# Conformer norm of a decoder trunk: the statistic as four columns, one unit further down, with some of its squares added on GpSimd

## The chip, the cores and the metric

One NeuronCore of a Trainium2 chip runs the whole kernel. The metric is the device time of one execution in microseconds; the time before is the median of three runs. A core has five engines that matter here: PE (TensorE; its weight loads are listed as PEld), DVE (VectorE), ACT (ScalarE), POOL (GpSimd) and SP (SyncE, which here only issues DMAs).

## The reference, cut to what matters

The reference is a trunk of two layers over 512 positions with 1024 channels. Layer 0 mixes tokens with a gated DeltaNet, layer 1 with a Conformer convolution module; each layer then attends to a fixed memory and applies a squared-ReLU MLP. Every sub-layer has an RMS norm before it and a residual add behind it.

```
def rms_norm(x, g):
    y = xf * lax.rsqrt(jnp.mean(xf * xf, axis=-1, keepdims=True) + RMS_EPS)
    return (y * g).astype(x.dtype)

def conformer_conv(h, w_pw1, b_pw1, w_dw, b_dw, ln_g, ln_b, w_pw2, b_pw2):
    u = h @ w_pw1 + b_pw1
    u = u[..., :D_MODEL] * jax.nn.sigmoid(u[..., D_MODEL:])
    c = causal_depthwise_conv(u, w_dw) + b_dw
    c = jax.nn.silu(layer_norm(c, ln_g, ln_b))
    return c @ w_pw2 + b_pw2
```

The change concerns the RMS norm ahead of `conformer_conv`: the mean over 1024 channels of h squared, for each of 512 tokens.

## The kernel before, in words

Activations lie with channels on the 128 partitions and the 512 tokens along a tile: a layer's state h is eight tiles of 128x512. Each operand of a matmul is split into a rounded part and a remainder (xh and xl, wh and wl; type fp32r), and a product is three matmuls of 512 columns, `mm3` (L290: lines 292, 293, 294). A projection `proj` (L300) runs `mm3` over the eight k tiles into one PSUM bank: 24 matmuls, called a unit here.

The norm's gain is folded into xh and xl (`Norm.parts`, L376: xh on ACT, xl on DVE). Its scale per token, rb, comes later: the projections run on unscaled x, and the result is multiplied by rb when it is taken out of PSUM. `Norm.square` (L383) squares an h tile on ACT (sq) and adds it to the running sum; the last add is on DVE. When all eight are in, `split` (L329) makes sqh and sql. `Norm.stat` (L395) multiplies both by a 128x128 matrix of ones, which sums over the partitions and leaves the sum in all 128 rows (ssq), takes the root of all 128x512 on ACT (sd) and the reciprocal on DVE (rb). Another way stands in the class and serves the first norm of the kernel: `stat_tok` (L404) takes root and reciprocal of a column for each 128 tokens (128x4, rstd), and `spread` (L410) spreads the four columns by four PE transposes (`spread_t`, L359) and a copy on ACT to rb.

The stretch in question is the end of layer 0's MLP and the start of the Conformer. `outs` (L1183) transposes the MLP's result back: four PSUM banks hT by 16 transposes, then for each tile h = hT + residual on DVE and `parts`. It is called for tiles 0 to 3 ahead of the last product of the MLP, and for tiles 4 to 7 (`rest`) inside the Conformer's first unit. Behind tile 7 it squares all eight h, with the adds on DVE.

`conformer` (L1266) begins with the first pointwise projection. `pw_mm` (L1274) runs unit (m, half): half 0 is the value and half 1 the gate of channel tile m. Unit (0, 0) does k 0 to 3, then `rest`, then unit (0, 1) does k 0 to 3, then both do k 4 to 7; inside the last of these, behind k = 5, stands `norm.stat`. `pw_ev` (L1285) scales by rb, applies the sigmoid and makes the gated tile: the sigmoid on ACT, the rest on DVE. Then come the convolutions: tile 0 has its 31 taps on ACT and GpSimd (cvp, ca), tiles 1 to 4 on DVE (L1350, one instruction for a tap), tiles 5 to 7 on PE (L1413). The projections of the memory's keys and values (K, V) fill PE meanwhile, in the order of `CONV_SEQ` and `CONV_AFTER` (L1732). The LayerNorm is taken on DVE (L1391 to L1438), and `ln_out` (L1442) transposes back on PE (lnT) for the second pointwise projection.

The order of the instructions on each engine is fixed when the kernel is built: a scheduler goes by the order of the program and by its own estimate of when operands are ready, so neighbouring units may be mixed. Each engine then runs its list strictly in that order and waits on semaphores. Weights come as raw tiles by SP's DMAs; `wsplit` (L241) makes wh on ACT and wl on DVE (some on GpSimd) two units ahead, in a ring of three (NW). PSUM has eight banks.

Of the kernel before, what the change touches and what calls it, by code (L numbers as in the profile page):

```python
# [11 lines left out]
ALU = mybir.AluOpType  # L12
AX = mybir.AxisListType

P = 128
# [22 lines left out]
def tile_trunk(ctx, tc, xT, memT, x_d, mem_d, prm_d, adt_d, bdw_d, tap_d, fin_d, w_ab, w_kq, w_v, w_z, w_dno, w_pw1, w_pw2,  # L38
               w_q, w_k, w_vv, w_o, w_up, w_dn, yT):
    nc = tc.nc  # L40
    pe, act, dve, pool = nc.tensor, nc.scalar, nc.vector, nc.gpsimd
# [10 lines left out]
    def nm(s):  # L52
        cnt[0] += 1
        return f"{s}_{cnt[0]}"

    def slot(dt=F32, s="u", shape=(P, NT)):
        return up.tile(list(shape), dt, tag="u", name=nm(s))

    def psum(s="ps"):
        return psp.tile([P, NT], F32, tag="ps", name=nm(s))  # L60
# [4 lines left out]
    def const(shape, s, dt=F32):  # L65
        return cp.tile(list(shape), dt, tag=s, name=s)
# [3 lines left out]
    def tt(e, o, a, b, op):  # L70
        r = e.tensor_tensor(out=o, in0=a, in1=b, op=op)  # L71
        if e is pool:
            last_pool[:] = [r]
        return r

    def stt(o, a, s, b, op0, op1):
        return dve.scalar_tensor_tensor(out=o, in0=a, scalar=s, in1=b, op0=op0, op1=op1)  # L77
# [7 lines left out]
    def c4(t):  # L85
        return t.rearrange("p (c i) -> p c i", c=4)
# [9 lines left out]
    def pc(name, i=0):  # L96
        return (gn0 if name == "dn_norm" else prm)[:, OFF[name] + i:OFF[name] + i + 1]
# [28 lines left out]
    ones = const([P, P], "ones")  # L126
# [137 lines left out]
    def wnext(key, hf):  # L264
        i = ws["next"]
        assert order[i] == (key, hf), (order[i], key, hf)
        while ws["load"] <= need[min(i + NRAW + 1 + 2 * (order[i][0][0] in ("up", "dn7")), len(order) - 1)]:
            wload()
        while ws["split"] < min(i + (NW if i > 2 else (1, 2, 2)[i]), len(order)):
            wsplit()  # L270
        ws["next"] += 1
        return ws["hl"].pop(i)
# [17 lines left out]
    def mm3(ps, wk, xk, first, last):  # L290
        (wh, wl), (xh, xl) = wk, xk
        pe.matmul(ps, wh, xh, start=first, stop=False)  # L292
        pe.matmul(ps, wh, xl, start=False, stop=False)  # L293
        pe.matmul(ps, wl, xh, start=False, stop=last)  # L294

    def wk(w, k):
        c = slice(k * P, (k + 1) * P)
        return w[0][:, c], w[1][:, c]

    def proj(w, xs, ps, k0=0, k1=KT, inside=None):  # L300
        for k in range(k0, k1):
            mm3(ps, wk(w, k), xs[k], k == 0, k == KT - 1)
            if inside and k in inside:
                inside[k]()
# [24 lines left out]
    def split(src, s):  # L329
        h = slot(F32R, s + "h")  # L330
        act.copy(h, src)  # L331
        lo = slot(F32R, s + "l")
        tt(dve, lo, src, h.bitcast(F32), ALU.subtract)
        return h, lo
# [32 lines left out]

    class Norm:
        def __init__(self, gname):
            self.g, self.acc, self.xs, self.n = gname, None, [], 0  # L370

        def add(self, t, h):
            self.parts(t, h)
# [6 lines left out]
            pin(stt(xl, h, pc(self.g, t), xh.bitcast(F32), ALU.mult, ALU.subtract))  # L380
            self.xs.append((xh, xl))

        def square(self, h, e=pool):  # L383
            sq = slot(s="sq")
            act.activation(sq, h, AF.Square)  # L385
            self.n += 1
            if self.acc is None:
                self.acc = sq
            else:
                tt(dve if self.n == KT else e, self.acc, self.acc, sq, ALU.add)  # L390
            if self.n == KT:
                self.hl = split(self.acc, "sq")

        def stat(self):
# [676 lines left out]
    def mlp7(layer, norm, hres, nxt=None, mid=None):  # L1071
        xs = norm.xs
# [108 lines left out]
        new = [None] * 8  # L1181

        def outs(tiles):  # L1183
            todo = [(n, c, i) for n in range(2) for c in range(2) for i in tiles]
            pss = {i: psum("hT") for i in tiles}
            for n, c, i in todo:
                j = 2 * n + c
                pe.transpose(pss[i][:, j * P:(j + 1) * P], acc[n, 1 - i // 4, c][:, i % 4 * P:i % 4 * P + P], ident)
            for k, i in enumerate(tiles):
                hn = slot(s="h")  # L1190
                tt(dve, hn, pss[i], hres[i], ALU.add)
                new[i] = hn
                if k:
                    nxt.parts(i - 1, new[i - 1])
            nxt.parts(i, hn)
            if i == 7:
                for hn in new:
                    nxt.square(hn, dve)

        def final(n, m, c):  # L1200
            opens = n not in fin or fin[n][4][c] is None
# [26 lines left out]
        for g in range(4):  # L1228
            ops, us = [{} for _ in range(4)], []
            for i in range(8):  # L1230
                w = wnext(("up", layer, g * 4 + i // 2), i % 2)
                ps = psum("up")
# [33 lines left out]
    def conformer(norm, hres, nxt, rest):  # L1266
        xs = norm.xs
        st, xg = {}, {}
        bn = slot(s="bn")
        Y = [[slot(s="cy") for _ in range(2)] for _ in range(4)]  # L1270
        for y in Y:
            nc.sync.dma_start(out=y[1], in_=bdw_d[512:1024].partition_broadcast(P))

        def pw_mm(m, hf):  # L1274
            w, st[m, hf] = wnext(("pw1", m), hf), psum("pw")
            if m:
                return proj(w, xs, st[m, hf])
            proj(w, xs, st[m, hf], 0, 4)
            if hf == 0:
                st["w"] = w  # L1280
                return rest()
            proj(st.pop("w"), xs, st[0, 0], 4, 8)
            proj(w, xs, st[0, 1], 4, 8, inside={5: norm.stat})

        def pw_ev(m):  # L1285
            sg = slot(s="sg")
            tt(dve, sg, st.pop((m, 1)), norm.rb, ALU.mult)
            act.activation(sg, sg, AF.Sigmoid, bias=pc("b_pw1", 8 + m))
            a = slot(s="pa")
            tt(dve, a, st.pop((m, 0)), norm.rb, ALU.mult)  # L1290
            if m == 0:
                x4 = c4(wp.tile([P, 544], F32, tag="cv", name=nm("xp"), bufs=NCV))
                pool.memset(x4[:, :, 0:8], 0.0)
                stt(x4[:, :, 8:136], c4(a), pc("b_pw1", m), c4(sg), ALU.add, ALU.mult)
                todo_p.extend(pool_conv(m, x4))
                return
            if m < NTAP:
                x7 = fsp.tile([P, 1024], F32, tag="fs", name=nm("x7"))[:, 0:1008].rearrange("p (q t) -> p q t", q=7)
                pool.memset(x7[:, :, 0:10], 0.0)
                stt(x7[:, 3:7, 8:136], c4(a), pc("b_pw1", m), c4(sg), ALU.add, ALU.mult)  # L1300
                act.copy(x7[:, 0:3, 9:137], x7[:, 4:7, 8:136])
                todo.extend(dve_conv(m, x7))
                return
            x = wp.tile([P, 544], F32, tag="cv", name=nm("xg"), bufs=NCV)
            x4 = c4(x)
            pool.memset(x4[:, :, 0:8], 0.0)
            gl = slot(s="glu")
            stt(gl, a, pc("b_pw1", m), sg, ALU.add, ALU.mult)
            for j in range(4):
                for b in range(4):  # L1310
                    nc.sync.dma_start(out=x4[32 * b:32 * b + 32, j, 8:136],
                                      in_=gl[32 * j:32 * j + 32, 128 * b:128 * b + 128])
            xg[m] = x4
# [64 lines left out]
        def taps_pool(n):  # L1378
            for _ in range(min(len(todo_p), n)):
                todo_p.pop(0)()  # L1380

        def taps_dve(n):
            for _ in range(min(len(todo), n)):
                todo.pop(0)()
# [76 lines left out]
        for i, (kind, u) in enumerate(CONV_SEQ):  # L1461
            if kind == "p":
                m, hf = divmod(u, 2)
                pw_mm(m, hf)
                if hf == 1:
                    pw_ev(m)
            else:
                kv_unit(1, u)

            for ins in gate:  # L1470
                stack.enter_context(tc.issue_after(ins.ins))
            taps_dve(TAPS_U[i])
            stack.close()
            taps_pool(2 if kind == "p" else 1)
            for what, m, *js in after.pop(i, ()):
                {"t": taps, "c": lambda m: conv(m, js), "l": lambda m: ln(), "s": lambda m: root_table(), "o": ln_out, "d": turn,
                 "m": lambda m: behind(first["tap"], moments, m)}[what](m)
                if what == "c":
                    for ins in gate:
                        stack.enter_context(tc.issue_after(ins.ins))  # L1480
                    taps_dve(TAPS_C[m])
                    stack.close()
                taps_pool(3 if what == "c" else 0)
            gate = [x for x in (ws["ins"], mem.get("kf")) if x is not None] if i >= 15 else []
        assert not after
        new = []
        for m in range(8):
            ps = psum("pw2")
            proj(wnext(("pw2", m // 2), m % 2), ss, ps)
            hn = slot(s="h")  # L1490
# [114 lines left out]
    for gq in range(2):  # L1605
# [9 lines left out]
        for i in range(4):  # L1615
            h = 4 * gq + i
# [50 lines left out]
    h = []  # L1667
# [13 lines left out]
    h = xattn(0, n1, h, n2)  # L1681
    n3 = Norm("cv_norm")
    h, rest = mlp7(0, n2, h, n3, lambda: (mem_gain(1, 0), mem_gain(1, 1), taps(NTAP)))
    n4 = Norm("xa_norm1")
    h = conformer(n3, h, n4, rest)
    n5 = Norm("mlp_norm1")
    h = xattn(1, n4, h, n5)
# [149 lines left out]
```

## Time and profile before

| | |
|---|---|
| runs, us | 1472.95, 1472.52, 1470.46 (median 1472.52) |
| profiled execution, us | 1472.31 |
| its span, us | 1470.6 |
| granted TensorE clock, mean of the span | 0.998 |
| DVE add `h<-hT,h`, 8 in the kernel | 684 ns each |
| DVE reciprocal of 128x512 (L401), 5 in the kernel | 3353 ns each |

The profile is taken from one execution. The span is from its first to its last instruction; the time of the execution also has what lies around it. Busy times are per engine; PE's matmuls are pipelined, so the distance between starts (0.23 us for 512 columns) and not the listed duration (0.39) is what one costs in a stream. A row gives start, duration, engine, line, operation and tiles (out<-in); in brackets stands how long the engine sat idle before it, and what ended that. Lists of a tile give duration in ns as min/median/max. Line numbers are those of the kernel before.

### The profile page before, as it was taken

The page shows a single profiled execution, that of the slowest core. Times are in us where ns is not written, and L with a number is a line of the kernel's source. Part 1 is how long each engine was busy: PE and PEld are TensorE (multiplying, and loading weights), DVE is VectorE, ACT ScalarE, POOL GpSimd, SP SyncE. Part 2 cuts the span into 40 slices and gives each one's busy share as a digit, 9 for nine tenths or more (in the row PEclk, how much of TensorE's full clock was granted, in tenths as well). Part 3 has the DMA queues.
Part 4 walks back from the last instruction along what each step waited for, and adds up shares of the span by engine and source line. Part 5 has one row for each costly group of instructions (what it writes and reads, how often), then busy time and mean ns, then how long its engine had stood idle before and what let it go on. Part 6 is the DMA issues. An engine that isn't in the chain of part 4 may idle for free.

```text
span 1470.6 us, 19621 instructions
## 1 busy us (share of the span) xinstructions
PE 1454.7 (99%) x7298; PEld 1226.6 (83%) x7298; DVE 1068.6 (73%) x1619; ACT 771.8 (52%) x1326; POOL 261.0 (18%) x285
## 2 busy tenths in 40 slices
PE   9999999999999999999999899999999999999998
PEld 7888889988888888888888689988888888888886
DVE  5889889867646766767679799985555766767677
ACT  7765865655434554444354655464444544444354
POOL 1411310103113000000000387302113000000100
PEclk9999999999999999999999999999999999999999
DMA  7232124342213666574766424432204466574853
GB/s 272 94 115 72 58 86 156 131 144 87 73 43 114 158 172 175 142 201 136 203 163 219 151 87 164 171 139 101 72 34 131 138 170 179 138 212 126 232 144 86
DMA packets 62736, 201.83 MB, mean 137 GB/s; under 512 B 7728, under 2 KB 10032, under 8 KB 62640
## 3 DMA queue, kind: packets, MB, share of 16 engines
q1 hardware_dynamic: 52416, 164.39, 31.7%
q0 software_dynamic: 9792, 35.66, 14.0%
q8 instruction: 57, 0.93, 0.2%
q10 hardware_dynamic: 432, 0.52, 0.1%
q14 instruction: 39, 0.32, 0.1%
HBM read 197.66 MB, written 2.10 MB: 136 GB/s over the span
## 4 chain that ended last, share of the span: by engine, by line
PE 92%; DVE 3%; ACT 2%; DMA 1%; issue 1%; SPq 0%; POOL 0%; DVEq 0%; ACTq 0%
PE up L294 8%; PE up L293 8%; PE up L292 8%; PE dn L1123 6%; PE dn L1121 6%; PE dn L1122 6%; PE pw L293 3%; PE pw L294 3%; PE pw L292 3%; PE h L292 2%; PE h L293 2%; PE h L294 2%; PE xo L293 2%; PE q L292 2%; PE q L293 2%; PE q L294 2%
## 5 line engine op out<-in xcount | busy, mean ns | idle before, releaser
L251 ACT CAST wh<-raw 128x1024 fp32r<-128x1024 f32 x259 | 272.0, 1052 | 356.5 <-issue 96.7
L71 DVE TENSOR_TENSOR wl<-raw,wh 128x1024 fp32r<-128x1024 f32 (+1 forms) x250 | 305.7, 1225 | 104.1 <-ACT wh L251 98.2
L292 PE MATMUL up<-xh,wh 128*128 128x512 f32 x512 | 199.7, 390 | 0.0
L294 PE MATMUL up<-xh,wl 128*128 128x512 f32 x512 | 199.3, 389 | 0.0
L293 PE MATMUL up<-xl,wh 128*128 128x512 f32 x512 | 199.2, 389 | 0.0
L293 PEld LDWEIGHTS up<-xl,wh 128*128 128x128 f32 x512 | 96.1, 188 | 20.0
L294 PEld LDWEIGHTS up<-xh,wl 128*128 128x128 f32 x512 | 96.1, 188 | 19.9
L292 PEld LDWEIGHTS up<-xh,wh 128*128 128x128 f32 x512 | 96.1, 188 | 19.8
L239 POOL DMA_DIRECT2D t<-w_dn x48 | 42.2, 917 | 360.9 <-DVE wl L71 239.8
L1121 PE MATMUL dn<-wh,ah 128*128 128x512 f32 x256 | 99.8, 390 | 0.0
L1123 PE MATMUL dn<-wl,ah 128*128 128x512 f32 x256 | 99.6, 389 | 0.0
L1122 PE MATMUL dn<-wh,al 128*128 128x512 f32 x256 | 99.6, 389 | 0.0
L77 DVE SCALAR_TENSOR_TENSOR rl<-up,rb 128x512 f32<-128x512 f32 x64 | 44.2, 690 | 58.2 <-PE up L294 58.2
L1350 DVE SCALAR_TENSOR_TENSOR ca<-x,prm,ca 128x512 f32<-128x512 f32 x112 | 82.3, 754 | 3.6 <-ACT ca L1347 1.3
L251 ACT CAST wh<-t 128x1024 fp32r<-128x1024 f32 x44 | 46.5, 1056 | 55.5 <-PE dn L1122 43.7
L71 DVE TENSOR_TENSOR wl<-t,wh 128x1024 fp32r<-128x1024 f32 x44 | 53.7, 1224 | 29.2 <-ACT wh L251 29.1
L292 PE MATMUL h<-xh,wh 128*128 128x512 f32 x184 | 73.7, 400 | 0.0
L294 PE MATMUL h<-xh,wl 128*128 128x512 f32 x184 | 71.9, 391 | 0.0
L293 PE MATMUL h<-xl,wh 128*128 128x512 f32 x184 | 71.7, 390 | 0.0
L71 DVE TENSOR_TENSOR acc<-acc,dn 128x512 f32<-128x512 f32 x100 | 67.4, 683 | 1.1
L71 POOL TENSOR_TENSOR sq<-sq,sq 128x512 f32<-128x512 f32 x24 | 39.1, 1631 | 147.4 <-ACT sq L385 137.0
L71 DVE TENSOR_TENSOR al<-u,ah 128x512 fp32r<-128x512 f32 x64 | 44.1, 688 | 21.4 <-ACT ah L331 21.4
(385 smaller groups left out, 3567.2 us busy)
## 6 DMA issues: line engine op xcount, KB each, us to landing
raw<-w_dn SPq DMA_DIRECT2D x68, 512.0 KB, 3.6
raw<-w_up SPq DMA_DIRECT2D x64, 512.0 KB, 4.7
t<-w_dn POOLq DMA_DIRECT2D x48, 512.0 KB, 5.7
raw<-w_pw SPq DMA_DIRECT2D x24, 512.0 KB, 3.8
raw<-w_dn POOLq DMA_DIRECT2D x20, 512.0 KB, 5.8
raw<-w_k SPq DMA_DIRECT2D x16, 512.0 KB, 3.4
raw<-w_vv SPq DMA_DIRECT2D x16, 512.0 KB, 4.4
t<-w_dn SPq DMA_DIRECT2D x16, 512.0 KB, 4.4
```

What stands on the lines that cost most here:

```text
L71: r = e.tensor_tensor(out=o, in0=a, in1=b, op=op)
L77: return dve.scalar_tensor_tensor(out=o, in0=a, scalar=s, in1=b, op0=op0, op1=op1)
L239: nc.gpsimd.dma_start(out=t, in_=a, accum_op=ALU.add)
L251: ins = [act.copy(h, raw)]
L292: pe.matmul(ps, wh, xh, start=first, stop=False)
L293: pe.matmul(ps, wh, xl, start=False, stop=False)
L294: pe.matmul(ps, wl, xh, start=False, stop=last)
L1121: pe.matmul(ps, xh, w[0][:, s], start=opens and k == 0, stop=False, skip_group_check=True)
L1122: pe.matmul(ps, xl, w[0][:, s], start=False, stop=False, skip_group_check=True)
L1123: pe.matmul(ps, xh, w[1][:, s], start=False, stop=k == 3, skip_group_check=True)
L1350: first["tap"] = dve.scalar_tensor_tensor(out=a, in0=src, scalar=w, in1=a, op0=ALU.mult, op1=ALU.add)
```

## The change

The eight squares of the Conformer's norm are no longer taken together behind tile 7. The squares of tiles 0 to 3 are taken behind the first `outs`, during the MLP's last product, and added up on GpSimd. Of the late tiles, 4 and 5 are squared between the `parts` of the tiles that follow, and added to each other on GpSimd in a sum of their own (`side`); 6 and 7 are added to the first sum on DVE, and then the side sum too. The sum isn't split into sqh and sql any more.

`columns` takes the place of `stat`: four float32 products, each with a 128x128 block of the sum as the stationary operand and one column of ones, give the sum for 128 tokens as a column, 128x4 in all; `stat_tok` and `spread` follow, as in the first norm. In the program `columns` stands behind k = 2 of unit (1, 0) and `spread` behind k = 4 of it, where `stat` stood behind k = 5 of unit (0, 1). `pw_ev(0)` is called behind `spread`, inside unit (1, 0), no longer behind unit (0, 1).

In the built lists, PE has unit (1, 0)'s first two matmuls mixed into the 24 that m = 0 has left (k 4 to 7), the columns behind its ninth matmul and the transposes eight matmuls later, one ahead of the last of k = 5. DVE loses five instructions on balance (four adds, the remainder sql; the reciprocal stays, on 128x4), GpSimd gains four adds of 128x512, ACT loses the cast sqh, has the root on 128x4, and gains the copy to rb. Behind that, DVE's and SP's lists have the old order; on ACT the scaled copies for GpSimd's taps stand in another order among the weights' casts.

```diff
 class Norm:
+        def columns(self):
+            ps = psum("ssq")
+            for c in range(4):
+                pe.matmul(ps[:, c:c + 1], self.acc[:, c * P:(c + 1) * P], ones[:, 0:1], start=True, stop=True)
+            self.stat_tok(ps[:, 0:4])
+
-        def square(self, h, e=pool):
+        def square(self, h, e=pool, side=False):
             sq = slot(s="sq")
             act.activation(sq, h, AF.Square)
             self.n += 1
+            if side:
+                if self.side:
+                    tt(pool, self.side, self.side, sq, ALU.add)
+                self.side = self.side or sq
+                return
             if self.acc is None:
                 self.acc = sq
             else:
                 tt(dve if self.n == KT else e, self.acc, self.acc, sq, ALU.add)
             if self.n == KT:
+                if self.side:
+                    tt(dve, self.acc, self.acc, self.side, ALU.add)
+                    return
                 self.hl = split(self.acc, "sq")
...
                 if k:
                     nxt.parts(i - 1, new[i - 1])
+                if i > 5:
+                    nxt.square(new[i - 2], side=True)
             nxt.parts(i, hn)
-            if i == 7:
-                for hn in new:
-                    nxt.square(hn, dve)
+            for hn in new[0:4] if i == 3 else new[6:8]:
+                nxt.square(hn, pool if i == 3 else dve)
...
+        def scale():
+            norm.spread()
+            pw_ev(0)
+
+        STAT = {2: norm.columns, 4: scale}
+
         def pw_mm(m, hf):
             w, st[m, hf] = wnext(("pw1", m), hf), psum("pw")
             if m:
-                return proj(w, xs, st[m, hf])
+                return proj(w, xs, st[m, hf], inside=STAT if (m, hf) == (1, 0) else None)
...
             proj(st.pop("w"), xs, st[0, 0], 4, 8)
-            proj(w, xs, st[0, 1], 4, 8, inside={5: norm.stat})
+            proj(w, xs, st[0, 1], 4, 8)
...
-                if hf == 1:
+                if hf == 1 and m:
                     pw_ev(m)
```

More of the change, by code (lines that the diff above doesn't have):

```diff
@@ L369, in __init__ @@
         def __init__(self, gname):
-            self.g, self.acc, self.xs, self.n = gname, None, [], 0
+            self.g, self.acc, self.xs, self.n, self.side = gname, None, [], 0, None
         def add(self, t, h):
```

## The prediction

> **What bounds the kernel now.** I read the page first: the span, and the shares of the chain that ended last.
>
> ```profile
> span 1470.6 us, 19621 instructions
> ...
> PE 92%; DVE 3%; ACT 2%; DMA 1%; issue 1%; SPq 0%; POOL 0%; DVEq 0%; ACTq 0%
> ```
>
> PE is the bound almost everywhere, so an edit elsewhere is worth what it takes from PE's pauses. The second view is the waits of PE, of which this is the longest (total, times, longest):
>
> ```profile
> PE ssq L397 <- ACT sqh L331: 4.5, 1, 4.5
> ```
>
> It is one wait, at the matmul of a norm's statistic (L397); five norms run that line, and only one waits so. The third view is PE's timeline around it (start, duration, in brackets the idle time before):
>
> ```profile
> 816.47 0.39 PE L294 MATMUL pw<-xh,wl 128*128 128x512 f32 x1
> 821.39 0.50 PE L397 MATMUL ssq<-sqh,ones_r 128*128 128x512 f32 x1 [4.54 <-ACT sqh L331]
> ...
> 823.07 0.63 PE L293 MATMUL pw<-xl,wh 128*128 128x512 f32 x1
> 823.50 0.63 PE L294 MATMUL pw<-xh,wl 128*128 128x512 f32 x1
> ...
> 828.00 0.39 PE L292 MATMUL pw<-xh,wh 128*128 128x512 f32 x1
> ...
> 836.84 0.39 PE L292 MATMUL pw<-xh,wh 128*128 128x512 f32 x1
> ```
>
> This is the start of the Conformer layer. From 828.00 to 836.84 lie 39 starts, 0.2267 us each: the steady pace. From 816.47 to 828.00 there are 21 starts, 4.76 us at that pace; they took 11.53. **The pause costs 6.77 us**: 4.54 of idle time, and 2.2 behind it, where matmuls are 0.43 apart (823.07, 823.50).
>
> What PE waited for is read in the timelines of ACT and of DVE:
>
> ```profile
> 804.90 0.72 ACT L378 ACTIVATE xh<-h,prm 128x512 fp32r<-128x512 f32 x1
> 809.07 1.34 ACT L378 ACTIVATE xh<-h,prm 128x512 fp32r<-128x512 f32 x2 [3.45 <-DVE h L71]
> ...
> 813.11 4.26 ACT L385 ACTIVATE sq<-h 128x512 f32<-128x512 f32 x8
> ...
> 820.72 0.62 ACT L331 CAST sqh<-sq 128x512 fp32r<-128x512 f32 x1 [1.47 <-DVE sq L71]
> ```
>
> ```profile
> 812.36 1.63 DVE L77 SCALAR_TENSOR_TENSOR xl<-h,prm,xh 128x512 fp32r<-128x512 f32 x2
> 814.28 4.67 DVE L71 TENSOR_TENSOR sq<-sq,sq 128x512 f32<-128x512 f32 x6 [0.29 <-ACT sq L385]
> 818.87 1.22 DVE L71 TENSOR_TENSOR wl<-raw,wh 128x1024 fp32r<-128x1024 f32 x1
> 820.00 0.69 DVE L71 TENSOR_TENSOR sq<-sq,sq 128x512 f32<-128x512 f32 x1
> ```
>
> All eight squares come after the last xh; then seven adds in a row, six of them 0.78 us each (4.67 / 6), the last behind a weight's wl; then the cast sqh. PE had run out of other matmuls at 816.7.
>
> **The change part by part.** *Removed from PE*: the pause, 6.77, and two 512-column matmuls, 2 x 0.2267 = 0.45. Together 7.22 us, if nothing new is late.
>
> *Added on PE*: four one-column float32 products with a 128x128 stationary, and four transposes. The nearest rows, from PE's timeline and from the list of the tile mg:
>
> ```profile
> 23.93 0.39 PE L294 MATMUL h<-xh,wl 128*128 128x512 f32 x1
> 24.16 0.60 PE L362 MATMUL rb<-ident,rstd 128*128 128x128 f32 x4
> 24.51 0.48 PE L292 MATMUL h<-xh,wh 128*128 128x512 f32 x1
> 24.83 0.39 PE L293 MATMUL h<-xl,wh 128*128 128x512 f32 x1
> ...
> 895.14 1.95 PE L1413 MATMUL cv<-tap,xg 128*128 128x128 f32 x16
> ```
>
> ```profile
> L682 PEld LDWEIGHTS mg<-x,bt x64: 187/192/192, 121.7 to 257.4; 128*128 128x128 f32 x64
> ```
>
> The transposes are those of the first norm (L362): from 23.93 to 24.83 is 0.90 where two plain matmuls take 0.45, so four cost 0.45. A one-column float32 product is nowhere in the trace. The nearest is L1413, same stationary and type: its 8 products of one block are 16 records, so a product is two, and four products are eight. Sixteen took 1.95, 0.122 each: 8 x 0.122 = 0.98. From below: four records at the price of transposes, 0.45. From above: eight loads of 0.192 (L682) with nothing beside them, 1.54. A cost below nothing is excluded, since PE is full here and has them in addition. I take 0.98.
>
> *Is the column sum in time?* By the order of instructions as built, PE does the same matmuls as before up to 816.47 (a little mixed), then nine of m = 1, then the first column: 816.47 + 10 x 0.2267 = 818.7. On ACT the four early squares stand behind the xh of 804.90, in the 3.45 us that ACT sat idle before 809.07 (4 x 0.53, from the row of eight, is 2.1: hidden). The four late ones stand between and behind the later xh, the last done by about 815.5. GpSimd does three adds of the early squares and one of the late ones; DVE has three adds left.
>
> ```profile
> L71 POOL TENSOR_TENSOR sq<-sq,sq x24: 1298/1758/1823, 347.4 to 1129.4; 128x512 f32<-128x512 f32 x24
> ```
>
> ```profile
> 836.64 3.63 POOL L71 TENSOR_TENSOR ca<-ca,cvp 128x512 f32<-128x512 f32 x2 [0.57 <-ACT cvp L1333]
> ```
>
> ```profile
> 837.34 1.78 DVE L77 SCALAR_TENSOR_TENSOR x<-pa,prm,sg 128x512 f32<-128x512 f32 x1
> ```
>
> A GpSimd add takes 1.30 at the least and 1.76 in the median. The pair at 836.64 shows why: a DVE instruction that reads two SBUF tiles begins inside a GpSimd add and takes 1.78, where its like (the two xl at 812.36) take 0.8 each. They block one another. So I let them take turns: GpSimd from 807.7 (two squares done at 806.6, one wl of DVE's in the way), each of DVE's four xl held up by at most one add of 1.30. The fourth xl then ends near 815.7 instead of 813.99, and three adds of 0.78 end at 818.0. PE wants the sum at 818.7: **in time by 0.7**. The third xl comes about 815.0 where PE's order would want it at 814.85; that and the like I price at 0.25 us of PE.
>
> The Trainium skill, page "SBUF — State Buffer", section "Who interferes with whom", calls this an exclusive lock: a DVE instruction with two SBUF inputs and a GpSimd instruction that reads SBUF block one another for a whole instruction, and issue order decides who waits. The trace agrees (1.78 against 0.8). By that rule the adds put on GpSimd do not free DVE for as long as they last; what that can cost is the first rival, and in the conv stage the second.
>
> *Behind the column sum*: a square root and a reciprocal of four columns, the transposes, a copy to rb.
>
> ```profile
> 22.37 0.30 ACT L405 ACTIVATE sd<-ss,eps_rms 128x4 f32<-128x4 f32 x1
> ```
>
> ```profile
> 22.70 0.18 DVE L407 RECIPROCAL rstd<-sd 128x4 f32<-128x4 f32 x1 [1.66 <-ACT sd L405]
> ```
>
> The columns end about 819.7 and land 0.3 later; 0.30 and 0.18 and the hand-overs give rstd at 820.7 (two wl of 1.22 stand ahead of it on DVE, done by 820.4). PE has eight matmuls, 1.8 us, between columns and transposes, until 821.5: hidden, with 0.8 to spare. Who waits for rb is DVE's gate of m = 0, and the units behind it need that only for their PSUM banks: ssq and rb hold two more for a few microseconds, while the four of hT are free again. SP's order of DMAs is the same as before.
>
> *Does the layer pass the gain on?* DVE is nearly full from here to the LayerNorm's transposes (columns of the first row: length, then busy PE, PEld, DVE, ACT, POOL; the second says what lnT's matmuls waited for):
>
> ```profile
> 840.00:960.00 120.00, 120.00 (x739) 107.56 (x738) 115.61 (x170) 64.32 (x115) 75.31 (x47) 1.00 0.41 145
> ```
>
> ```profile
>   DVE cy L83: 0.3, 1
> ```
>
> PE waits 0.3 us there for DVE's last normalization: both arrive together, and PE's gain counts only if DVE comes earlier too. It does: its taps start behind the gate of m = 1, which waits for that unit's end on PE, and that end moves with PE. The work behind it is the same, in the same order on DVE.
>
> *Sum*, against the profiled execution (1472.31 us: 1470.6 of span and 1.7 around it): 1472.31 - 7.22 + 0.98 + 0.45 + 0.25 = **1466.8**. That execution lies 0.2 below the median of the runs shown, 1472.52; I make no correction.
>
> **The rivals.** *R1, the wait moves.* The column sum comes late through the blocking: four GpSimd adds at 1.76 instead of 1.30, all handed on to DVE, are 1.84 more against 0.7 of slack. PE waits 1.1, which gives 1467.9. For it: the slack is less than one add. Against: GpSimd's adds of early squares run while DVE mostly reads PSUM (hT), where no two SBUF tiles are read. It is also the way in which the change does only part of what it says.
>
> *R2, the gain is lost at lnT.* The blocking strikes in the conv stage too (DVE's timeline):
>
> ```profile
> 904.24 2.31 DVE L71 TENSOR_TENSOR wl<-raw,wh 128x1024 fp32r<-128x1024 f32 x1
> ...
> 931.45 2.21 DVE L71 TENSOR_TENSOR wl<-raw,wh 128x1024 fp32r<-128x1024 f32 x1
> ```
>
> Against the 1.22 of an undisturbed wl, 1.09 and 0.99, and 1.0 at 837.34: some 3.1 us of DVE. The order in which ACT feeds GpSimd's taps changes, so where the two meet changes. As many strikes again cost 3.1 at lnT: 1469.9, hardly to be told from no change. Against: the present ones may as well go.
>
> *R3, slower.* The same place, further. Some eleven DVE instructions with two SBUF inputs (x and glu, wl, Kl) stand in the stage while GpSimd works. If eight more are blocked, 1.1 each, DVE's end comes 8.8 later than I count: 1475.6. It decides the sign from the point where DVE's chain is longer by 5.5 us, all that was gained. For it: at 115.6 of 120 us DVE can make nothing up. Against: three strikes in the present stage, not eleven.
>
> **How the numbers follow.** Forecast 0.62, R1 0.18, R2 0.15, R3 0.05. About 0.2%, 2.9 us, is what a measurement of this kernel can tell from no change: faster (below 1469.4: forecast and R1) 0.80, within 0.15, slower 0.05. The range: below, columns at 0.45, no xl late, and 1.2 for half the spread of the runs before (1470.46 to 1472.95): 1464.8; above, columns at 1.54 and most of R2: 1470.2.
>
> **What would show it.** Right: no wait of microseconds on PE near 817 and matmuls 0.23 apart throughout; the eight column records within 1 us; lnT about 5.5 us earlier, waiting less than 0.5 for DVE. Wrong: PE waiting at ssq for DVE or GpSimd (R1); lnT waiting microseconds for cy, with DVE rows of 1.8 to 2.4 in the conv stage (R2, R3).

## The result, and the profile after

| | before | after |
|---|---|---|
| median, us | 1471.47 | 1465.58 |
| lowest to highest, us (six runs each) | 1470.46 to 1472.95 | 1465.09 to 1466.23 |
| ratio of after to before | | 0.9959, 95% interval 0.9946 to 0.9972 |
| profiled execution, us | 1472.31 | 1465.73 |
| its span, us | 1470.6 | 1463.9 |
| granted TensorE clock | 0.998 | 0.999 |

The kernel is 5.9 us faster; 1466.8 was forecast, with 1464.8 to 1470.2 as the range. Line numbers of the kernel after differ: `columns` is L386, the squares L391, `stat_tok` L419 and L421, the taps of DVE L1371, lnT L1466.

This is the whole list of PE's waits after (total, times, longest):

```profile
PE warm L130 <- POOL ones L127: 1.2, 1, 1.2
PE abT L459 <- DVE ab L71: 0.6, 1, 0.6
PE dt L543 <- DVE L L77: 0.2, 1, 0.2
PE rb L362 <- DVE rstd L421: 0.2, 1, 0.2
PE dn L1137 <- DVE wl L71: 0.2, 1, 0.2
```

The wait of 4.5 us at ssq is gone and nothing of its size has come instead; the one at rb belongs to the first norm of the kernel, at 23.2. PE's timeline where it was:

```profile
817.49 0.39 PE L294 MATMUL pw<-xh,wl 128*128 128x512 f32 x1
817.71 0.95 PE L386 MATMUL ssq<-ones,sq 128*128 128x1 f32 x8
818.52 0.49 PE L292 MATMUL pw<-xh,wh 128*128 128x512 f32 x1
818.85 0.40 PE L293 MATMUL pw<-xl,wh 128*128 128x512 f32 x1
...
820.24 0.39 PE L293 MATMUL pw<-xl,wh 128*128 128x512 f32 x1
820.47 0.60 PE L362 MATMUL rb<-ident,rstd 128*128 128x128 f32 x4
820.82 0.48 PE L294 MATMUL pw<-xh,wl 128*128 128x512 f32 x1
821.14 0.39 PE L292 MATMUL pw<-xh,wh 128*128 128x512 f32 x1
```

The four column products are eight records, as expected. From 817.49 to 818.85 is 1.36 where two plain matmuls take 0.45: they cost **0.91**. From 820.24 to 821.14 is 0.90 for the same two: the transposes cost **0.45**. In the listed stretch no bracket stands: PE never idles.

What feeds the columns is read in the timelines of POOL and of DVE:

```profile
805.94 3.36 POOL L71 TENSOR_TENSOR sq<-sq,sq 128x512 f32<-128x512 f32 x2
...
809.38 1.62 POOL L71 TENSOR_TENSOR sq<-sq,sq 128x512 f32<-128x512 f32 x1
811.81 1.29 POOL L71 TENSOR_TENSOR sq<-sq,sq 128x512 f32<-128x512 f32 x1 [0.80 <-ACT sq L391]
```

```profile
808.83 1.02 DVE L77 SCALAR_TENSOR_TENSOR xl<-h,prm,xh 128x512 fp32r<-128x512 f32 x1 [0.20 <-ACT xh L378]
...
810.38 1.18 DVE L77 SCALAR_TENSOR_TENSOR xl<-h,prm,xh 128x512 fp32r<-128x512 f32 x1
...
812.08 2.23 DVE L77 SCALAR_TENSOR_TENSOR xl<-h,prm,xh 128x512 fp32r<-128x512 f32 x2
814.23 2.27 DVE L71 TENSOR_TENSOR sq<-sq,sq 128x512 f32<-128x512 f32 x3
816.77 2.36 DVE L71 TENSOR_TENSOR wl<-raw,wh 128x1024 fp32r<-128x1024 f32 x2 [0.27 <-ACT wh L251]
819.05 0.17 DVE L421 RECIPROCAL rstd<-sd 128x4 f32<-128x4 f32 x1
821.72 0.69 DVE L71 TENSOR_TENSOR sg<-pw,rb 128x512 f32<-128x512 f32 x1 [2.50 <-ACT rb L427]
```

GpSimd's adds take 3.36 for the first two together, then 1.62 and 1.29. The blocking of DVE and GpSimd is there, but smaller than allowed for: the four xl take 1.02, 1.18 and 2.23 for the last two, against 0.75 to 0.8 each. The sum is done at 816.5 (814.23 + 2.27), **1.2 us** ahead of the columns. The last row is the gate of m = 0, the first instruction that needs rb.

At the other end of the stage, the matmuls of lnT; the second row is what they waited for:

```profile
L1466 PE MATMUL lnT<-ident,cy x32: 270/272/329, 959.0 to 968.3; 128*128 128x128 f32 x32
...
  DVE cy L83: 0.3, 1
```

Two executions don't start alike, so I measure from a common mark, the start of the last group of hT transposes: 807.27 before, 806.28 after. The first lnT starts 158.59 us behind it before and 152.75 after: **5.84 us are gained in this stage**. The spans of the two profiled executions differ by 6.7. The rest of that is 1.0 gained before the mark, where PE's work is the same, less 0.1 lost behind lnT. The 1.0 is no part of the change: PE's list of before has a wait of 1.2 at 8.4, for an xh of the kernel's first projection, which the list of after hasn't. The medians differ by 5.89.

### The profile page after: what moved, and what is told of

Same layout as the page of the kernel before. It is cut to its first block, busy times and chain, and to the rows that moved or that the text cites. A ratio compares the mean times of both kernels' runs of the same rounds, so it can differ in the third digit from the quotient of the medians.

```text
span 1463.9 us, 19643 instructions
## 1 busy us (share of the span) xinstructions
PE 1453.6 (99%) x7308; PEld 1226.7 (84%) x7308; DVE 1061.2 (72%) x1614; ACT 770.8 (53%) x1326; POOL 266.2 (18%) x289
## 4 chain that ended last, share of the span: by engine, by line
PE 93%; DVE 3%; ACT 2%; DMA 1%; issue 0%; SPq 0%; POOL 0%; DVEq 0%; ACTq 0%
PE up L294 8%; PE up L292 8%; PE up L293 8%; PE dn L1137 6%; PE dn L1136 6%; PE dn L1135 6%; PE pw L292 3%; PE pw L294 3%; PE pw L293 3%; PE h L292 2%; PE h L293 2%; PE h L294 2%; PE xo L293 2%; PE q L293 2%; PE xo L294 2%; PE q L292 2%
## 5 line engine op out<-in xcount | busy, mean ns | idle before, releaser
L1371 DVE SCALAR_TENSOR_TENSOR ca<-x,prm,ca 128x512 f32<-128x512 f32 x112 | 82.3, 752 | 3.6 <-ACT ca L1368 1.3
L71 POOL TENSOR_TENSOR sq<-sq,sq 128x512 f32<-128x512 f32 x28 | 45.4, 1620 | 148.3 <-ACT sq L391 137.8
```

What stands on the lines that cost most here:

```text
L1371: first["tap"] = dve.scalar_tensor_tensor(out=a, in0=src, scalar=w, in1=a, op0=ALU.mult, op1=ALU.add)
```

## The experiments

My theory after the result: PE is the bound; the gain is the pause, and it comes because the statistic's chain, once short enough and far enough down, ends in time. What was open: which part of the change is needed, and whether DVE, at 115.6 of 120 us busy, really had nothing to spare.

### The place alone

```diff
+        def scale():
+            norm.stat()
+            pw_ev(0)
+        STAT = {7: scale}
-                return proj(w, xs, st[m, hf])
+                return proj(w, xs, st[m, hf], inside=STAT if (m, hf) == (1, 0) else None)
...
-            proj(w, xs, st[0, 1], 4, 8, inside={5: norm.stat})
+            proj(w, xs, st[0, 1], 4, 8)
...
-                if hf == 1:
+                if hf == 1 and m:
```

This is the kernel before with its late squares and its old statistic, put at the end of unit (1, 0).

> One part alone: the statistic as before (sqh, sql, ones, root and reciprocal of 128x512; all eight squares late, added on DVE), only moved down to the end of unit (1, 0), with the gate of m = 0 behind it. Theory (the gain is PE's pause and nothing else): PE reaches the statistic 25 matmuls later, at about 822.1 on the clock of the profile before, where sqh was ready at 821.3 and sql at 822.4; the pause shrinks to 0.1 to 0.3 us, the two matmuls stay: 6.4 to 6.7 us faster than before, so 0.5 to 0.8 faster than the change as made. Rival (the late chain on DVE counts): rb comes behind a reciprocal of 3.35 us, the gates of m = 0 and 1 and with them DVE's taps begin over 1 us later relative to PE, and lnT waits for DVE: 5 us faster or less, with lnT waiting 1 us or more for cy.

Measured: 1469.28 against 1471.88, ratio 0.9984 (0.9976 to 0.9993): 2.6 us, far from what the theory had, and without what the rival gave as its reason: lnT waits 0.3, as before. The pause at ssq is gone. But PE has a new wait, in the pointwise projection (PE's timeline):

```profile
856.92 0.39 PE L293 MATMUL pw<-xl,wh 128*128 128x512 f32 x1
860.21 0.80 PE L294 MATMUL pw<-xh,wl 128*128 128x512 f32 x1 [2.90 <-POOL wl L71]
```

PE waits for the remainder of a weight that GpSimd makes, 50 us behind the mark. The suspicion: rb is late. The root and the reciprocal run on 128x512 here (3.35 us the reciprocal), so DVE's gate of m = 0 begins 20.5 us behind the mark (829.01 and 808.49 in this profile), against 15.4 in the change; the tap products of ACT wait for the gate, GpSimd's taps wait for those, and its wl stand in line behind the taps. That is tested further down.

### The early squares alone

```diff
-                    return
                 self.hl = split(self.acc, "sq")
...
-                return proj(w, xs, st[m, hf], inside=STAT if (m, hf) == (1, 0) else None)
+                return proj(w, xs, st[m, hf])
...
-            proj(w, xs, st[0, 1], 4, 8)
+            proj(w, xs, st[0, 1], 4, 8, inside={5: norm.stat})
...
-                if hf == 1 and m:
+                if hf == 1:
```

The change with the old statistic at its old place; only the early squares and GpSimd's adds stay.

> One part alone: the squares early and partly on GpSimd, as in the change; statistic with sqh, sql and 128x512 root and reciprocal, at its old place. Theory: the sum is ready when the three DVE adds end, 816.5 in the profile after, which is 817.5 on the clock of the one before; the cast makes it 818.2, PE arrives at 816.7 and waits 1.5 us, sql hides behind the matmuls between, and a wait this short leaves no slow matmuls behind: 5.0 to 5.3 us faster than before. Rival (any pause of over a microsecond slows the matmuls behind it as the long one did): 2 us more are lost, 3 us faster.

Measured: 1469.61 against 1471.88, ratio 0.9985 (0.9976 to 0.9994): 2.3 us, less than the theory had; the rival's 3 lies in the interval. PE's timeline:

```profile
816.03 0.39 PE L294 MATMUL pw<-xh,wl 128*128 128x512 f32 x1
818.39 0.50 PE L410 MATMUL ssq<-sqh,ones_r 128*128 128x512 f32 x1 [1.97 <-ACT sqh L331]
...
820.80 0.39 PE L294 MATMUL pw<-xh,wl 128*128 128x512 f32 x1
```

A pause of 1.97 stays, and ACT shows why: sqh stands behind two casts of a weight that come late.

```profile
815.82 1.99 ACT L251 CAST wh<-raw 128x1024 fp32r<-128x1024 f32 x2 [1.72 <-issue]
817.72 0.61 ACT L331 CAST sqh<-sq 128x512 fp32r<-128x512 f32 x1
```

From 816.03 to 820.80 are 11 starts, 2.49 at the steady pace; they took 4.77. So this pause costs 2.28 in all, 0.31 more than its idle time, and the matmuls behind it are not slow: the rival's reason isn't in this profile. In this profile lnT starts 154.76 behind the mark, 3.8 earlier than before; the medians give only 2.3. In the profiled execution 1.0 of that is lost again behind PE's last matmul: from its end to the end of the span are 8.35 us, against 7.33 before. Where the other 0.5 lies is open.

### The columns at the old place

```diff
-        STAT = {2: norm.columns, 4: scale}
+        STAT = {0: scale}
...
-            proj(w, xs, st[0, 1], 4, 8)
+            proj(w, xs, st[0, 1], 4, 8, inside={5: norm.columns})
```

> The change with the columns at the old place (behind k = 5 of unit (0, 1)) and the transposes behind k = 0 of unit (1, 0). Theory: PE wants the columns at 816.7 on the clock of before, the sum is ready at 817.5: a wait of 0.8; rstd needs about 1.3 us from the end of the columns and PE has six to seven matmuls, 1.5 us: 5.0 us faster than before, 0.9 slower than the change. Rival (being further down is what makes the gain): 3 us faster or less.

Measured: 1467.01 against 1471.88, ratio 0.9967 (0.9954 to 0.9979): 4.9 us, as the theory had it. The columns need no split, so they need not wait for ACT, and begin at 816.78. But the loss is not the one wait of 0.8 that the theory had (PE's timeline):

```profile
813.40 0.39 PE L292 MATMUL pw<-xh,wh 128*128 128x512 f32 x1
813.93 0.50 PE L293 MATMUL pw<-xl,wh 128*128 128x512 f32 x1
...
816.78 1.05 PE L386 MATMUL ssq<-ones,sq 128*128 128x1 f32 x8 [0.27 <-DVE sq L71]
```

At the columns PE loses 0.55 beyond their cost (1.91 us from the matmul ahead of them, 816.11, to the second behind, 818.02, less 0.45 and 0.91). Another 0.41 goes at 813.93: that matmul reads an xl, and DVE's third xl is done just ahead of it, at 813.87, held up by a GpSimd add that ends at 813.32. Together 0.96; lnT starts 0.99 later than in the change.

### The late squares with the columns further down

```diff
-                if self.side:
-                    tt(dve, self.acc, self.acc, self.side, ALU.add)
+                if self.g == "cv_norm":
                     return
...
-                if i > 5:
-                    nxt.square(new[i - 2], side=True)
...
-            for hn in new[0:4] if i == 3 else new[6:8]:
-                nxt.square(hn, pool if i == 3 else dve)
+            if i == 7:
+                for hn in new:
+                    nxt.square(hn, dve)
```

All eight squares together behind tile 7, added on DVE as before the change.

> The change with all eight squares late and added on DVE, as before; columns and transposes down in unit (1, 0). Theory: the sum is ready at 820.7 on the clock of before; by the built order PE comes to the columns at about 820.5, so it waits 0.2 there, and the transposes hide behind six matmuls only just: 5.3 to 5.8 us faster than before. Rival (early squares and GpSimd carry the gain): a pause of 2 us and more stays, 3.8 us faster or less.

Measured: 1465.88 against 1471.88, ratio 0.996 (0.9948 to 0.9973): 6.0 us, all of the gain, and a little more than the theory's 5.3 to 5.8. In the built list the columns stand nine matmuls lower than in the change, and the sum, done at 821.13, is just in time for them at 821.18 (timelines of DVE and of PE):

```profile
820.44 0.69 DVE L71 TENSOR_TENSOR sq<-sq,sq 128x512 f32<-128x512 f32 x1
```

```profile
821.18 1.05 PE L386 MATMUL ssq<-ones,sq 128*128 128x1 f32 x8
```

So the early squares are one of two ways to be in time, and not needed beside the other.

### The same adds on DVE

```diff
-                    tt(pool, self.side, self.side, sq, ALU.add)
+                    tt(dve, self.side, self.side, sq, ALU.add)
...
-                nxt.square(hn, pool if i == 3 else dve)
+                nxt.square(hn, dve)
```

> The change with GpSimd's four adds put on DVE; PE's order is the same. Theory (GpSimd's adds neither gain nor cost, since the sum is in time either way): DVE's three early adds fit where it waited for hT or lie behind wl, the xl are no longer held up; sum ready within 0.7 us of the change's, PE without a wait: the time of the change within 0.3 us, 5.9 faster than before. Rival (the adds on GpSimd are what gets the sum in time): the sum is 2 us later or an xl is, PE waits over 0.5 us at ssq or in m = 0: over 0.5 slower than the change.

Measured: 1465.88 against 1471.69, ratio 0.9958 (0.9945 to 0.9972): 5.8 us, as the theory had it. In this order of work GpSimd's part neither gains nor costs. Without it the xl take 0.74 to 0.75 each again.

### The old statistic with early squares, further down

```diff
-                    return
                 self.hl = split(self.acc, "sq")
...
-            norm.spread()
+            norm.stat()
...
-        STAT = {2: norm.columns, 4: scale}
+        STAT = {2: scale}
```

> Early squares as in the change, but the statistic with sqh, sql and 128x512 root and reciprocal, behind k = 2 of unit (1, 0). Theory: by the built order PE comes to sqh some two matmuls behind where the change has its columns, 819.2 on the clock of before, and sqh is ready at 818.2: no wait; two matmuls of 0.23 in place of columns (0.91) and transposes (0.45): 6.6 to 6.8 us faster than before, 0.8 faster than the change. Rival (the 3.35 us reciprocal delays the gates and so DVE's taps): no faster than the change, with lnT waiting longer for DVE.

Measured: 1466.17 against 1471.69, ratio 0.996 (0.9947 to 0.9972): 5.5 us, not the theory's 6.6 to 6.8 and no better than the change; the rival's wait at lnT isn't there either (0.3 again). In the profile the first lnT starts 152.63 behind the mark, 0.12 earlier than in the change. PE's timeline shows what the saved 1.36 of columns and transposes went for:

```profile
818.06 0.39 PE L293 MATMUL pw<-xl,wh 128*128 128x512 f32 x1
818.39 0.50 PE L410 MATMUL ssq<-sqh,ones_r 128*128 128x512 f32 x1
...
822.22 0.39 PE L293 MATMUL pw<-xl,wh 128*128 128x512 f32 x1
...
854.86 0.39 PE L293 MATMUL pw<-xl,wh 128*128 128x512 f32 x1
855.47 0.50 PE L294 MATMUL pw<-xh,wl 128*128 128x512 f32 x1 [0.22 <-POOL wl L71]
...
856.03 0.40 PE L293 MATMUL pw<-xl,wh 128*128 128x512 f32 x1
```

From 818.06 to 822.22 stand 17 starts, 3.85 at the steady pace, in 4.16: with the two matmuls of ssq themselves (0.45) the statistic costs 0.76. From 854.86 to 856.03 three starts take 1.17 instead of 0.68: 0.49 more, for the same wl of GpSimd as in the first experiment. Together 1.25, against 1.36: a gain of 0.1.

### Useless work on DVE

Three, and nine, more tap instructions in tile 2's taps, with a result that nothing reads: work that the computation doesn't need.

```diff
+                if m == 2 and 10 <= d < 10 + EXTRA:
+                    dve.scalar_tensor_tensor(out=c4(st["junk"]), in0=src, scalar=w, in1=a, op0=ALU.mult, op1=ALU.add)
```

> The change with three useless DVE instructions more in the conv stage, like a tap (reads PSUM and SBUF, writes a tile that nothing reads), 0.75 us each: 2.26 us of DVE. What the prediction held (DVE and PE arrive together at lnT, DVE is the bound): lnT waits 2.2 us longer, 2.2 us slower than the change. Rival (DVE has slack: in the profile after it sat 2.1 us at 934.3 waiting for a cast that waits for PE): nothing, within 0.4 us of the change.

> The same with nine such instructions: 6.8 us of DVE. If DVE is the bound of the stage: 6.8 us slower than the change, 0.9 slower than before. If it has some 2 to 3 us of slack: 3.8 to 4.8 us slower than the change, with PE's wait moving to lnT or the transposes of the conv stage.

Measured: with three (2.26 us) 1465.9 against 1471.69, ratio 0.9959 (0.9945 to 0.9972), the change's own; with nine (6.8 us) 1470.88, ratio 0.9997 (0.9988 to 1.0006), 5.0 more, a little above the 3.8 to 4.8 that slack of 2 to 3 us would leave. So DVE had at least 2.3 us to spare, and less than 6.8. The second bound is the weaker one: with three PE's list is that of the change, but with nine it is another from 962 on, and nine more matmuls stand ahead of the first lnT. With nine it is again a weight of GpSimd's that stops PE first, ahead of that place, and not lnT:

```profile
PE K L294 <- POOL wl L71: 3.0, 1, 3.0
```

Where DVE's spare time is, after, is one row of its timeline:

```profile
934.30 1.23 DVE L71 TENSOR_TENSOR wl<-raw,wh 128x1024 fp32r<-128x1024 f32 x1 [2.12 <-ACT wh L251]
```

It idles 2.12 us for a cast on ACT; with three useless taps the same wait is 1.46. ACT's timeline has the cast in question and the next one:

```profile
933.22 1.05 ACT L251 CAST wh<-raw 128x1024 fp32r<-128x1024 f32 x1 [1.10 <-issue]
...
936.06 1.05 ACT L251 CAST wh<-raw 128x1024 fp32r<-128x1024 f32 x1 [1.79 <-PE K L293]
```

The casts before it and behind it wait for PE's matmuls of K (4.99 and 1.79); for this one the profile names nothing. They come 2.8 to 3.3 us apart, about as PE's units of K do (24 matmuls, 0.12 us apart: 2.9). That DVE follows PE here is therefore likely, but not shown for this cast.

### A late gate

The first experiment once more for a second profile, and the change with one and with two useless reciprocals of 128x512 on DVE that read rb, ahead of the gate of m = 0.

```diff
             norm.spread()
+            for _ in range(LATE):
+                dve.reciprocal(slot(s="junk"), norm.rb)
             pw_ev(0)
```

> The kernel of the old statistic at the end of unit (1, 0), unchanged, for a second profile: the first was taken of its slowest execution (1473.16 us, median 1469.28). Theory: the wait of PE for a wl made by GpSimd, 2.9 us at 857 in the first profile, is part of this order of work and stands in every execution; what differs is how long PE then runs at half pace (5.6 us of 0.43-us matmuls in the first profile): the wait is again 2 to 3 us, and if the time is near the median, fewer slow matmuls stand behind it. Rival: the wait came from a disturbance of that one execution: no wait over 0.5 us, and the time still near 1469.

> The change, with one useless reciprocal of 128x512 (3.35 us) on DVE that reads rb and stands ahead of the gate of m = 0. Theory (a late rb costs through the gates: DVE's gate, the taps on ACT and GpSimd behind it, the weights' remainders that GpSimd makes behind its taps, PE): DVE idles 0.75 + 0.19 + 2.24 = 3.2 us between the gate of m = 0 and that of m = 1, so 3.35 us more are hidden: the time of the change within 0.5 us, no wait of PE over 0.5 us. Rival (any delay of rb goes on to PE in full): 3 us slower than the change.

> The same with two such reciprocals, 6.7 us. Theory: 3.2 hidden, 3.5 left; the taps of DVE begin 3.5 us later than in the change, as far behind the end of hT as in the kernel with the old statistic further down (29.7 us), and as there PE waits some 2.9 us in pw for a wl made by GpSimd, with or without slow matmuls behind it: 3 to 6 us slower than the change, 1468.5 to 1471.5. Rival (that kernel's wait came from the order of its own lists on ACT and PE, and a late gate is harmless as long as the LayerNorm has 2 us to spare): at most 1.2 us slower than the change.

Measured, against 1472.03: 1470.2 for the first (a single run); with one reciprocal 1466.69, ratio 0.9964 (0.995 to 0.9978); with two 1471.62, ratio 0.9997 (0.9988 to 1.0006). Against the change, whose gain was 5.89, that is 0.55 and 5.5 us lost: just outside the theory's 0.5, and the upper part of its 3 to 6 (the time itself lies 0.1 above the range given with it). The wait of the first experiment is there again. PE's timelines of the three, in this order:

```profile
858.50 0.50 PE L294 MATMUL pw<-xh,wl 128*128 128x512 f32 x1 [2.88 <-POOL wl L71]
```

```profile
856.49 0.50 PE L294 MATMUL pw<-xh,wl 128*128 128x512 f32 x1 [0.23 <-POOL wl L71]
```

```profile
859.72 0.50 PE L294 MATMUL pw<-xh,wl 128*128 128x512 f32 x1 [3.39 <-POOL wl L71]
```

Set beside each other, each from its own mark (start of DVE's gate of m = 0; start of DVE's taps; end of the wl on GpSimd; start that PE's matmul with this wl would have at the steady pace; PE's idle time there; start of lnT; us):

| kernel | gate | taps | wl done | wl due | wait | lnT |
|---|---|---|---|---|---|---|
| the change | 15.4 | 26.2 | 48.2 | 49.3 | none | 152.75 |
| early squares, old statistic further down | 18.3 | 27.0 | 49.0 | 48.7 | 0.22 | 152.63 |
| one reciprocal | 18.7 | 27.7 | 49.7 | 49.4 | 0.23 | 153.34 |
| old statistic further down | 20.5 | 29.7 | 51.7 | 48.7 | 2.90 | 158.14 |
| the same, again | 20.5 | 29.8 | 51.7 | 48.7 | 2.88 | 156.88 |
| two reciprocals | 22.0 | 31.0 | 52.9 | 49.4 | 3.39 | 158.07 |

The wait follows the gate, whatever makes the gate late: the theory holds. In all six the wl is done 21.9 to 22.0 us behind the start of DVE's taps, whatever the order of ACT's list, so that order is not needed to explain the first experiment's wait. PE's list has a small share in it: without columns and transposes PE comes to this matmul 0.7 earlier.

One link is other than the suspicion had it. Timelines of ACT and of POOL in the first experiment:

```profile
850.70 0.72 ACT L1294 ACTIVATE sg<-sg,prm 128x512 f32<-128x512 f32 x1 [8.24 <-DVE sg L71]
```

```profile
851.97 5.88 POOL L71 TENSOR_TENSOR ca<-ca,cvp 128x512 f32<-128x512 f32 x4 [4.33 <-ACT cvp L1341]
857.81 4.68 POOL L71 TENSOR_TENSOR wl<-raw,wh 128x1024 fp32r<-128x1024 f32 x2
```

The first of the two wl is done at 860.15, and PE goes on at 860.21. What ACT waits for is the gate of m = 2, which stands in DVE's list behind the first of its taps and begins 11.7 to 11.8 us behind their start. So the lateness goes on through DVE's own taps: gate of m = 0, taps, gate of m = 2, ACT's products, GpSimd's taps, wl, PE. Some 3 us of a late gate are hidden, 1.8 of them ahead of the taps and 1.1 between wl and PE; the rest stops PE.

## Why the prediction was right, point by point

- **The pause, 6.77, and two matmuls, 0.45: right.** With the measured costs the sum is -7.22 + 0.91 + 0.45 = -5.86; the stage shows -5.84.
- **Columns 0.98: measured 0.91.** The nearest row, the taps at 0.122 a record, carried; eight records was right. **Transposes 0.45: measured 0.45.**
- **Blocking of xl on PE, 0.25: measured nothing.** This is the mis-sized term of the sum. With the 0.07 of the columns it is all of the difference between -5.54 and -5.86. The blocking is real, but in the change PE's list comes to these xl late enough; with the columns at the old place it cost 0.41. The time of 1466.8 was 1.2 too late, and most of that is not the sum: it was added to an execution of 1472.31, where the median before is 1471.47, and that is 0.84.
- **The sum in time by 0.7: by 1.2.** The taking of turns was counted too dearly: of four GpSimd adds, 1.02 + 1.18 + 2.23 - 4 x 0.75 = 1.4 came through to DVE's xl, where 1.7 was allowed for. R1 didn't happen.
- **Behind the columns: right.** rstd is done at 819.2, the transposes start at 820.47: 1.2 to spare, 0.8 forecast. But "the units behind it need that only for their PSUM banks" failed: through DVE's gate, the taps and GpSimd's wl they need rb by a date, and the late-gate runs put that date some 3 us behind the change's. At its own rb the change doesn't feel it.
- **Passing the gain on: right in its result, wrong in its reason.** "Both arrive together" took the 0.3 at lnT as a sign that DVE was as late as PE. Three useless taps were swallowed: DVE had 2.3 us or more to spare. Its taps do start earlier, as said, 26.2 us behind the mark against 33.1. R2 and R3 rested on "DVE can make nothing up", and were priced too dearly by those 2.3.
- **The strikes of R2** changed place, as said, and cost less. In DVE's timeline after, the counterparts of the three rows quoted are

```profile
830.50 0.74 DVE L77 SCALAR_TENSOR_TENSOR x<-pa,prm,sg 128x512 f32<-128x512 f32 x1
...
896.70 1.23 DVE L71 TENSOR_TENSOR wl<-raw,wh 128x1024 fp32r<-128x1024 f32 x1
...
922.82 2.15 DVE L71 TENSOR_TENSOR wl<-raw,wh 128x1024 fp32r<-128x1024 f32 x1
```

Two of three are gone, and those that stand elsewhere instead cost 0.3 us or less each. That is no part of the gain either, as the useless taps show.

What the prediction did not ask is which part of the change does it. By the runs: the columns with early squares, at the old place, give 4.9 of the 5.9; the columns further down give all of it, with early or late squares; the old statistic gives 2.3 with early squares alone, 2.6 when it alone is put further down (to the end of unit (1, 0)), and 5.5 with both. GpSimd's share gives nothing beside columns further down. Between the change and the versions that tie with it (ratios of 0.9958 to 0.996) these runs can't tell.

## What to carry to other kernels

A statistic that PE waits for can be put further down, or its chain made shorter; what counts is that each of its dates holds, and a scale has two of them: the one at which PE's own matmul wants its operand, and the one at which the consumers of the result, here gates and taps with a weight's remainder in line behind them, hold up PE some thirty microseconds behind the gate. A busy share of 96% and a wait of 0.3 us at the end do not show that an engine has nothing to spare: a few useless instructions on it do, or a row of its own idle time. Where four 128x1 columns will do, the root and the reciprocal run on 128x4, and 3.35 us become 0.17.

## What the runs showed of the hardware

How much a pause of PE costs beyond its idle time isn't settled by its length; it goes with the clock granted behind it. Behind the 4.54 of before the clock was 0.57 from 821.30 to 825.20, where the prediction has its matmuls 0.43 apart, and behind the 3.39 of two reciprocals 0.51 from 860.70 to 864.20. The windows behind four other pauses (stretch, its length, busy times of PE, PEld, DVE, ACT, POOL, granted clock, DMA share, GB/s), first the old statistic further down (2.90 idle), then the same again (2.88), then nine useless taps (3.00), then early squares alone (1.97):

```profile
860.10:866.30 6.20, 6.09 (x14) 4.79 (x15) 6.20 (x11) 3.79 (x7) 5.94 (x5) 0.50 0.49 172
```

```profile
860.00:863.00 3.00, 3.00 (x9) 2.36 (x8) 3.00 (x5) 2.73 (x7) 2.75 (x3) 0.52 0.71 253
```

```profile
939.30:942.00 2.70, 2.68 (x22) 2.68 (x23) 1.71 (x2) 0.00 (x0) 0.00 (x0) 1.00 0.64 170
```

```profile
818.30:821.00 2.70, 2.61 (x11) 2.18 (x12) 2.25 (x3) 0.72 (x2) 0.00 (x0) 1.00 0.60 194
```

Twice the clock was at half behind the pause, for some 6 us and for some 3, and twice it stayed at full speed, once behind the longest of these four. That is why two executions of one kernel with the same wait reached lnT 1.3 us apart (158.14 and 156.88): the pause cost 6.1 us in the one (17 starts in 9.92 us) and 4.8 in the other (14 in 7.95). It may also be why kernels that keep a pause spread more from run to run (1467.47 to 1473.16) than the change does (1465.09 to 1466.23). The Trainium skill, page "TensorE: Matmul & The Clock Gate", section "What's actually happening", has a window of about 3.4 us that runs freely and isn't started by the kernel; by that the place of a pause in the window would decide. The trace agrees in that 2.88 and 3.00 us of idle time had different outcomes; the windows themselves are not seen in it. The Trainium skill asks for an idle window as a whole, though, and here 2.9 us of idle time were enough.
